# Where the background steps of a modulation stand, and which engine normalises v, in a two-layer retention and gMLP backbone

## The chip, the cores and the metric

The kernel runs on one core of one Trainium2 chip. The metric is the device time of one execution in microseconds, as the median of several runs. Engines are called PE (TensorE, the matmuls), DVE (VectorE), ACT (ScalarE), POOL (GpSimd) and SP (SyncE, which issues most DMA loads). Each engine works through its own instructions in order and waits on semaphores for the others.

## The reference

512 latent tokens and 256 context tokens of width 1024 go through two layers. Layer 0 is a retention mixer with four heads (query and key width 256, value width 512) in both directions, in which latents read context and latents. Layer 1 is a gMLP with spatial gating. Only the latents are put out, after a last RMS norm.

```python
shift, scale, gate = split(silu(c) @ ada_w[i] + ada_b[i], 3)       # per layer, 1024 each
hx = rmsnorm(x, norm_g[i]) * (1 + scale) + shift
# layer 0: q, k, v, z = hx @ w_in; retention in both directions; out = (rmsnorm(o) * silu(z)) @ w_out
# layer 1:
u, v, z = hx @ w_in                                              # 2048 each
v = v - mean(v); v = v * rsqrt(mean(v * v) + eps) * vnorm_g
mixed = einsum('gij,bnjgc->bnigc', w_s, v in chunks of 128) + b_s
out = (u * mixed * silu(z)) @ w_out
x = x + gate * out
```

## The kernel before

Everything is float32. A product is made as three matmuls of rounded halves (`mm3`): an operand is cast by ACT to its high half and DVE subtracts that from the original to get the low half (`split`, tiles `hl` for weights, `ya` and `og` for activations, `ph`/`pl` for scores). So every weight tile of 128x1024 costs one ACT cast and one DVE subtraction before PE can use it. The 2x2 block products of the projections are further made by a scheme with seven sub-products instead of eight (names B11, T1, T2, B21, T3, B22, T4 in `SINGLE`; a T is a difference of two raw weight tiles, a DVE subtraction `raw<-raw` ahead of its split). `Stream` (the object `Q`) loads the raw tiles and makes the splits two products ahead of PE.

The stages, with their rough times in the profile: start and layer 0's modulation (to 60 us); the projections of layer 0, nine unpaired groups ("quads") `n` of seven products each after a first one and a pair (to 350 us); attention over four heads, each followed by its part of the output projection (to 561 us); the v projection of layer 1 (to 640 us), which spills v to DRAM; then eight gating quads `i` with u and z, with an output product `out1` behind every second one (to 901 us).

*Order.* PE's instructions keep the order of the text. On DVE and ACT the framework's scheduler orders them by its own costs, except those made inside `aside(...)` (line 812): these are pinned behind the instruction that the text has ahead of them on their engine. SP issues loads in an order that the scheduler sets, each one waiting for its tile to be free; a waiting load holds those behind it.

*Background pieces.* Layer 1's modulation needs four vectors that come from 1024x1024 blocks of its matrix: the gate of layer 0 (piece 0), shift (1), scale (2) and the gate of layer 1 (3). `ada_piece` (line 745) makes one: nine loads' worth of steps in which tiles `bg` of 512 KB are loaded a step ahead, DVE multiplies the first by a column (`ada_a<-bg,cpad`, a TENSOR_SCALAR) and adds seven more (SCALAR_TENSOR_TENSOR). `background` (line 781) runs the pieces one after the other; each takes twelve steps: 1 loads only, 2 to 9 have one DVE instruction of 128x1024, 10 is empty, 11 and 12 turn the row into columns (`columns`: two small matmuls, an ACT copy `cole`, four transposes, a DVE copy), or for piece 3 load the bias (11) and add two 128x512 parts (12). One call of `step()` makes one step.

Steps are called in three places: in the loop over the projection quads (lines 925 to 939: product `i` of 7; five per quad until three pieces are done), in `attend` (line 947; `i` counts score pairs with the value product two behind, 0 to 7; three per head) and in `project_out` (line 1037; three per head).

*A head.* `score` makes the scores of a pair of blocks into one of two PSUM tiles `tm`, DVE scales them by the decay (`pf`), ACT casts (`ph`), DVE subtracts (`pl`). `pv` multiplies by v. At the end of a half of the tokens `finish` takes squares and their root on ACT (`junk`, `ss`), a DVE reciprocal and two `gt`; `flip` transposes `gt` on PE and splits it into `og`. At `i == 6` PE makes the value product of the fifth pair and then the transposes of the first half; at `i == 7` the value product of the sixth pair.

*Gating.* `bn_stats` and `bn_aggr` give mean and variance `mv` of v by token; `rv` is 1/sqrt(var + eps) (line 1220). `load_vt` (line 1286) loads a 256-column piece of v in two tiles `vt` of 128x2x256 and normalises it, four DVE instructions of 128x256; it is called at T2 of a gating quad for the next quad. After B22, sixteen matmuls mix v over tokens, and `gate_f` (line 1296) makes the gated product `ya`.

Of the kernel before, what the change touches and what calls it, by code (L numbers as in the profile page):

```python
# [9 lines left out]
AF = mybir.ActivationFunctionType  # L10
ALU = mybir.AluOpType
AX = mybir.AxisListType

P = 128
# [5 lines left out]
NT = SEQ // P  # L20
# [47 lines left out]
def hybrid_kernel(ctx, tc, xT_d, cT_d, cv_d, sv_d, rows_d, ada0_d, adag_d, w_d, rope_d, dec_d, ws_d, id_d, out_d):  # L68
    nc = tc.nc
    pe, act, dve, sp = (Queue(tc, e) for e in (nc.tensor, nc.scalar, nc.vector, nc.sync))  # L70
# [11 lines left out]
    def st(shape, tag, dt=F32, bufs=1, name=None):  # L82
        return sb.tile(shape, dt, tag=tag, name=name or tag, bufs=bufs)
# [37 lines left out]
    def pt(shape=(P, 512), tag="ps"):  # L121
        return ps.tile(list(shape), F32, tag=tag, name="pst", bufs=6 if tag == "ps" else 2)
# [21 lines left out]
    def load(dst, src):  # L144
        sp.dma_start(dst, src)
# [290 lines left out]
    g1 = sv[:, 72:80]  # L436
# [304 lines left out]
    def bg_raw(tags):  # L741
        spot[0] += 1
        return st([P, 1024], tags[spot[0] % len(tags)], name="bg")

    def ada_piece(i, tag, tags):
        a = st([P, D], tag, name="ada_a")
        rows = []
        for k in range(KT + 1):
            if k < KT:
                rows.append(bg_raw(tags))  # L750
                load(rows[k], adag_d[8 * i + k])
            if k == 0:
                yield None
                continue
            r, c = rows[k - 1], cpad[:, k - 1, 0:1]
            if k == 1:
                dve.tensor_scalar(a, r, c, None, ALU.mult)
            else:
                dve.scalar_tensor_tensor(a, r, c, a, ALU.mult, ALU.add)
            yield None  # L760
        yield a
# [19 lines left out]
    def background():  # L781
        for i in range(4):
            a = None
            for a in ada_piece(i, *(("g1", ("g2", "g3")) if i < 3 else ("oA22", ("w2", "w3")))):
                if a is None:
                    yield
            yield
            if i == 0:
                yield from columns(a, gate0)
                dve.tensor_tensor(gate0, gate0, gateb0, ALU.add)  # L790
            elif i == 1:
                yield from columns(a, sh1)
                dve.tensor_tensor(sh1, sh1, adab1[:, 0, :], ALU.add)
                dve.tensor_tensor(shs, sh1[:, 0:4], sh1[:, 4:8], ALU.add)
            elif i == 2:
                yield from columns(a, gs1)
                dve.tensor_tensor(gs1, gs1, adab1[:, 1, :], ALU.add)
                dve.scalar_tensor_tensor(gs1, gs1, 1.0, g1, ALU.add, ALU.mult)
            else:
                gb = st([P, D], "g1", name="gateb1")  # L800
                load(gb, rows_d[0:1, :].partition_broadcast(P))
                yield
                for j in range(2):
                    pr = pt(tag="tm")
                    mm(pr, ones, a[:, j * 512:j * 512 + 512], start=True, stop=True)
                    dve.tensor_tensor(gb[:, j * 512:j * 512 + 512], pr, gb[:, j * 512:j * 512 + 512], ALU.add)
                Q.gate = gb
            yield i
# [113 lines left out]
    pieces = []  # L922
    qk0 = load_qk(0)
    v0 = load_v(0)
    for n, q in enumerate(QUADS[3:]):
        pr = project(q)
        for i, name in enumerate(SINGLE):
            pr.run(name, Q.get())
            if i % 2:
                popped()  # L930
            if 2 not in pieces and i not in (2, 4):
                pieces.append(step())
            if n == 5 and i % 2 == 0:
                aside(dec0)
            if n >= 6:
                aside(qk0)
            if n == 8:
                aside(v0)
# [8 lines left out]
    def attend(h, qs, vs):  # L947
        q, k, kc = qk.pop(h)
        v, z = vv.pop(h)
        dt = dts[h]  # L950
        og = [st([P, 2, 4, HS], tag, F32R, name="og") for tag in ("oS3", "oS4")]
        steps = [(hf, j) for hf in range(2) for j in range(0, NK, 2)]
        ph, po, pend = {}, {}, []

        def key(j):
            return (k[j // 2], j % 2) if j < NT else (kc, j - NT)

        def score(hf, j):

            p = pt(tag="tm")  # L960
            for o in range(2):
                src, jj = key(j + 1 - o)
                for m in range(2):
                    l = (src[:, 0, m, jj * P:jj * P + P], src[:, 1, m, jj * P:jj * P + P])
                    mm3(p[:, o * HS:o * HS + HS], l, (q[hf][:, 0, m, :], q[hf][:, 1, m, :]), m == 0, m == 1)
            j1 = j + 1
            s0 = hf * HS - P * j1 + P * (NT - 1) if j < NT else XW + hf * HS - P * (j1 - NT) + P * (NC_T - 1)
            base = dt[:, s0:s0 + HS]
            both = bass.AP(base.tensor, base.offset, [base.ap[0], (P, 2), (1, HS)])
            two = lambda x: x.rearrange("p (o t) -> p o t", o=2)  # L970
            a = t2("pf")
            dve.scalar_tensor_tensor(two(a), two(p), 1.0 / 16.0, both, ALU.mult, ALU.mult)
            hl = t2("ph", dt=F32R), t2("pl", dt=F32R)
            split(hl, a)
            ph[hf, j] = hl

        def pv(hf, j):
            if j == 0:
                po[hf] = [pt(), pt()]
            h, l = ph.pop((hf, j))  # L980
            src = v[j // 2]
            for jj in range(2):
                for t in range(2):
                    o = (1 - jj) * HS + t * P
                    mm3(po[hf][t], (h[:, o:o + P], l[:, o:o + P]), (src[:, 0, jj, :], src[:, 1, jj, :]),
                        j + jj == 0, j + jj == NK - 1)
            if j == NK - 2:
                finish(hf)

        def finish(hf):  # L990
            ss = st([P, 2], "ss", bufs=2)
            for t in range(2):
                act.activation(t2("junk"), po[hf][t], AF.Square, accum_out=ss[:, t:t + 1])
            act.activation(ss, ss, AF.Sqrt, bias=eps, scale=1.0 / 512)
            dve.reciprocal(ss, ss)
            gts = []
            for t in range(2):
                g = t2("gt")
                dve.scalar_tensor_tensor(g, po[hf][t], ss[:, t:t + 1], z[:, 2 * hf + t, :], ALU.mult, ALU.mult)
                gts.append(g)  # L1000
            pend.append((hf, gts))

        def flip():
            hf, gts = pend.pop(0)
            for fp in range(2):
                pq = pt()
                for b in range(2):
                    for t in range(2):
                        o = b * HS + t * P
                        pe.transpose(pq[:, o:o + P], gts[t][:, (2 * fp + b) * P:(2 * fp + b) * P + P], ident)  # L1010
                src = pq.rearrange("p (b t) -> p b t", b=2)
                split((og[hf][:, 0, 2 * fp:2 * fp + 2, :], og[hf][:, 1, 2 * fp:2 * fp + 2, :]), src)

        LAG = 2
        wo = load_wo(h)
        for i in range(len(steps) + LAG):
            if i < len(steps):
                score(*steps[i])
            if i >= LAG:
                pv(*steps[i - LAG])  # L1020
            aside(qs)
            if i > 4:
                aside(vs)
            if i == len(steps):
                flip()
            if (h, i) == (0, 2):
                sp.pinned = True
                for c in range(4):
                    load(acc[:, 2 * c:2 * c + 2, :], xT_d[:, 2 * c:2 * c + 2, :])
                sp.pinned = False  # L1030
            if i < 5:
                aside(wo)
            if i in (3, 5, 6):
                step()
        return og, flip

# [180 lines left out]
    mv = st([P, NT, 2], "mv")  # L1217
    for t in range(NT):
        dve.bn_aggr(mv[:, t, :], bns[:, t, :, :])
    rv = st([P, NT], "rv")  # L1220
    act.activation(rv, mv[:, :, 1], AF.Sqrt, bias=eps, scale=1.0)
    dve.reciprocal(rv, rv)

    o1 = [st([P, D], f"s{t}", name="o1") for t in range(NT)]
    ya = st([P, 4, 2, SEQ], "hc", F32R, name="ya")
# [60 lines left out]
    def load_vt(i):  # L1286
        vts[i] = []
        for th in range(2):
            v = t2("vt", (P, 2, HS))
            load(v, vt_d[i][:, 2 * th:2 * th + 2, :])  # L1290
            for t in range(2):
                n = 2 * th + t
                dve.tensor_scalar(v[:, t, :], v[:, t, :], mv[:, n, 0:1], rv[:, n:n + 1], ALU.subtract, ALU.mult)
            vts[i].append(v)

    def gate_f(f, pm, mine):
# [144 lines left out]
```

## Time and profile before

| | |
|---|---|
| times of the runs | 908.04, 906.09, 906.26 us; median 906.26 |
| span of the profiled execution | 908.2 us |
| busy in it | PE 884.4 us (97%), DVE 720.0 (79%), ACT 445.8 (49%), POOL 51.4 (6%) |
| mean DMA rate | 168 GB/s over the span |
| commonest instruction groups | DVE split `hl<-raw,hl` 195 times, 1219 ns each; ACT cast `hl<-raw` 195 times, 1050 ns each |

The profile was taken of one execution; its span lies 0.2 us from the slowest of the three times and 1.9 from the median. Rows of a timeline read: start in us, duration in us, engine, line, operation, out<-in, shape, count, and in brackets how long the engine stood idle ahead of it and whose instruction ended that. All instructions show line 54, a helper; the tile names tell which is which. Consecutive instructions overlap a little, so from start to start is shorter than the duration (a 1.28 us instruction of 128x1024 takes 1.19 to the next start). PEclk is the granted clock of PE, 1.00 being full.

### The profile page before, as it was taken

The numbers are of one execution on the slowest core, as the hardware profiler recorded it, in microseconds if no ns is written. First come the engines' busy times: TensorE is split into PE (matmuls) and PEld (weight loads), VectorE is DVE, ScalarE is ACT, GpSimd is POOL, SyncE is SP. The second block draws the span as 40 slices with busy tenths as digits, with TensorE's granted clock in tenths as the row PEclk, the third lists the DMA queues.
The fourth block names the chain that finished last, engine by engine and source line by source line (L and its number), as shares of the span: only waits on it lengthen the run. The fifth ranks groups of instructions, "written<-read, shape, count | busy, mean of one in ns | idle before, by whom it ended". The sixth has DMA issues, their size and how long they took to land.

```text
span 908.2 us, 16915 instructions
## 1 busy us (share of the span) xinstructions
PE 884.4 (97%) x6872; PEld 839.3 (92%) x6872; DVE 720.0 (79%) x1024; ACT 445.8 (49%) x683; POOL 51.4 (6%) x88
## 2 busy tenths in 40 slices
PE   8999999999999999999999999999999999999986
PEld 7899999999999999998989898999999899899875
DVE  3689967698689876888677669999899478689975
ACT  5564634434445435626263558654445444353334
POOL 0001201101101011000000001111000000000000
PEclk9999999999999999999999999999999999999999
DMA  9933957467477458758253611636335035128002
GB/s 338 399 121 109 320 194 255 153 191 223 154 237 239 140 183 316 255 161 260 79 184 118 209 47 59 215 96 211 118 117 187 24 116 187 44 96 283 19 24 93
DMA packets 76782, 153.81 MB, mean 169 GB/s; under 512 B 7840, under 2 KB 34592, under 8 KB 76704
## 3 DMA queue, kind: packets, MB, share of 16 engines
q1 hardware_dynamic: 69840, 130.70, 44.2%
q0 software_dynamic: 6720, 22.03, 6.4%
q8 instruction: 54, 0.88, 0.4%
q14 instruction: 24, 0.20, 0.1%
q10 hardware_dynamic: 144, 0.01, 0.0%
HBM read 128.58 MB, written 24.12 MB: 168 GB/s over the span
## 4 chain that ended last, share of the span: by engine, by line
PE 67%; DVE 19%; DMA 5%; ACT 4%; issue 4%; SPq 1%; DVEq 0%; ACTq 0%
PE pst L54 67%; DVE hl L54 6%; DMA raw<-in_w_dram 3%; DVE raw L54 3%; DVE ya L54 2%; DVE o L54 2%; DVE snap L54 1%; SPq L54 1%; DMA vt<-vt 1%; DMA xq<-in_xT_dram 1%; ACT hl L54 1%; DVE f L54 1%; DVE pf L54 1%; ACT junk L54 1%; DVE oS L54 1%
## 5 line engine op out<-in xcount | busy, mean ns | idle before, releaser
L54 DVE TENSOR_TENSOR hl<-raw,hl 128x1024 fp32r<-128x1024 f32 x195 | 236.0, 1219 | 68.0 <-ACT hl L54 67.8
L54 ACT CAST hl<-raw 128x1024 fp32r<-128x1024 f32 x195 | 203.7, 1050 | 129.0 <-PE pst L54 71.2
L54 PE MATMUL pst<-oS,hl 128*128 128x256 f32 x1104 | 135.6, 282 | 4.6 <-DVE hl L54 3.9
L54 PE MATMUL pst<-hl,oS 128*128 128x256 f32 x1152 | 137.8, 281 | 2.0 <-DVE hl L54 1.8
L54 PEld LDWEIGHTS pst<-hl,oS 128*128 128x128 f32 x1152 | 135.8, 190 | 3.5 <-DVE hl L54 2.3
L54 PEld LDWEIGHTS pst<-oS,hl 128*128 128x128 f32 x1104 | 131.4, 190 | 6.9 <-ACT ya L54 3.7
L54 PE MATMUL pst<-oA,hl 128*128 128x256 f32 x936 | 117.5, 281 | 0.7 <-DVE snap L54 0.5
L54 PEld LDWEIGHTS pst<-oA,hl 128*128 128x128 f32 x936 | 112.2, 189 | 3.2 <-issue 1.3
L54 DVE TENSOR_TENSOR raw<-raw 128x1024 f32<-128x1024 f32 x92 | 111.4, 1218 | 1.2 <-DMA raw<-in_w_dram 0.5
L54 ACT COPY snap<-pst 128x512 f32<-128x512 f32 x92 | 53.9, 586 | 103.4 <-PE pst L54 102.9
L54 PE MATMUL pst<-hl,oA 128*128 128x256 f32 x816 | 98.6, 279 | 0.4 <-DVE snap L54 0.4
L54 PEld LDWEIGHTS pst<-hl,oA 128*128 128x128 f32 x816 | 96.3, 189 | 0.6 <-issue 0.6
L54 PE MATMUL pst<-og,hl 128*128 128x256 f32 x768 | 92.5, 281 | 0.0
L54 PEld LDWEIGHTS pst<-og,hl 128*128 128x128 f32 x768 | 90.4, 189 | 0.9 <-DVE acc L54 0.2
L54 PE MATMUL pst<-hl,ya 128*128 128x512 f32 x288 | 70.8, 399 | 2.7 <-DVE ya L54 2.7
L54 PEld LDWEIGHTS pst<-hl,ya 128*128 128x128 f32 x288 | 54.9, 192 | 15.2 <-DVE ya L54 3.1
L54 PE MATMUL pst<-v,ph 128*128 128x512 f32 x192 | 60.1, 395 | 0.0
L54 DVE TENSOR_TENSOR snap<-pst,snap 128x512 f32<-128x512 f32 x69 | 47.2, 684 | 3.9 <-PE pst L54 3.6
L54 ACT CAST ph<-pf 128x512 fp32r<-128x512 f32 x24 | 14.9, 621 | 67.1 <-DVE pf L54 66.7
L54 PE MATMUL pst<-hl,hc 128*128 128x256 f32 x384 | 47.4, 280 | 0.0
L54 PEld LDWEIGHTS pst<-hl,hc 128*128 128x128 f32 x384 | 46.0, 189 | 0.0
L54 PEld LDWEIGHTS pst<-v,ph 128*128 128x128 f32 x192 | 36.2, 188 | 7.3
(171 smaller groups left out, 970.3 us busy)
## 6 DMA issues: line engine op xcount, KB each, us to landing
raw<-in_w_dram SPq DMA_DIRECT2D x224, 256.0 KB, 4.4
bg<-in_adag_dram SPq DMA_DIRECT2D x32, 512.0 KB, 4.3
ada_w<-in_ada_dram SPq DMA_DIRECT2D x16, 512.0 KB, 8.7
raw<-in_w_dram SPq DMA_DIRECT2D x16, 512.0 KB, 4.3
bg<-in_dec_dram SPq DMA_DIRECT2D x12, 512.0 KB, 4.4
v<-snap POOLq DMA_DIRECT2D x16, 256.0 KB, 5.0
z<-snap POOLq DMA_DIRECT2D x16, 256.0 KB, 4.2
v<-v SPq DMA_DIRECT2D x8, 512.0 KB, 4.3
```

The source lines that it names most:

```text
L54: made = op(*args, **kw)
```

## The change

Five edits:

1. In `background`, the tiles `g1`, `g2`, `g3` serve pieces 0 and 1 only; piece 2 now uses `oA22`, `w2`, `w3`, as piece 3 does.
2. In the projection loop, steps are called at three products of a quad (0, 3, 5) instead of five (0, 1, 3, 5, 6), and until two pieces are done instead of three.
3. In `attend`, a step is called at every `i` from 2 to 7, six a head instead of three.
4. A new tile `nm` of 128x4 holds minus the mean times `rv`, by one DVE instruction.
5. `load_vt` normalises v by ACT (`Identity` with scale `rv` and bias `nm`) instead of DVE.

```diff
-            for a in ada_piece(i, *(("g1", ("g2", "g3")) if i < 3 else ("oA22", ("w2", "w3")))):
+            for a in ada_piece(i, *(("g1", ("g2", "g3")) if i < 2 else ("oA22", ("w2", "w3")))):
...
-            if 2 not in pieces and i not in (2, 4):
+            if 1 not in pieces and i in (0, 3, 5):
                 pieces.append(step())
...
-            if i in (3, 5, 6):
+            if i > 1:
                 step()
...
     dve.reciprocal(rv, rv)
+    nm = st([P, NT], "la", name="nm")
+    dve.scalar_tensor_tensor(nm, mv[:, :, 0], -1.0, rv, ALU.mult, ALU.mult)
...
-                dve.tensor_scalar(v[:, t, :], v[:, t, :], mv[:, n, 0:1], rv[:, n:n + 1], ALU.subtract, ALU.mult)
+                act.activation(v[:, t, :], v[:, t, :], AF.Identity, bias=nm[:, n:n + 1], scale=rv[:, n:n + 1])
```

In steps: before, pieces 0 to 2 end in the projection (at n = 7, i = 0), and piece 3 takes steps 1 to 3 in head 0, 4 to 6 in its output projection, 7 to 9 in head 1 and 10 to 12 behind it. After, piece 0 takes n = 0 to 3 and piece 1 n = 4 to 7; piece 2 takes steps 1 to 6 in head 0, 7 to 9 in its output projection and 10 to 12 in head 1; piece 3 takes 1 to 3 in head 1, 4 to 6 behind it and 7 to 12 in head 2.

## The prediction

> **What bounds the kernel now.** First the engine totals and PE's own waits, from the page and the list of waits.
>
> ```profile
> span 908.2 us, 16915 instructions
> PE 884.4 (97%) x6872; PEld 839.3 (92%) x6872; DVE 720.0 (79%) x1024; ACT 445.8 (49%) x683; POOL 51.4 (6%) x88
> ```
>
> ```profile
> PE pst L54 <- DVE hl L54: 5.7, 4, 2.0
> PE pst L54 <- DVE ya L54: 2.7, 1, 2.7
> PE pst L54 <- DVE pl L54: 1.7, 3, 0.7
> ```
>
> TensorE is the bound: 908.2 - 884.4 = 24 us idle in all, 10.1 of them in the three groups above, all released by DVE. Nothing in the change alters PE's work, only who prepares it, so only PE's waits can move: these and new ones. The prediction is a list of those waits. Second, the granted clock around the three longest waits (windows view: stretch, length, PE, PEld, DVE, ACT, POOL busy, PEclk, DMA share, GB/s), in stretches of 3.41 us.
>
> ```profile
> 221.44:224.85 3.41, 1.64 (x14) 1.44 (x14) 3.41 (x4) 1.60 (x3) 0.00 (x0) 1.00 0.74 258
> 224.85:228.26 3.41, 3.41 (x19) 3.41 (x18) 1.46 (x2) 0.00 (x0) 0.00 (x0) 0.50 0.83 190
> 658.34:661.75 3.41, 1.42 (x13) 1.25 (x12) 3.41 (x5) 3.41 (x6) 0.00 (x0) 1.00 0.00 0
> 661.75:665.16 3.41, 3.41 (x19) 3.41 (x18) 3.41 (x4) 0.83 (x1) 0.00 (x0) 0.50 0.23 61
> 747.08:750.49 3.41, 2.01 (x18) 1.83 (x17) 3.41 (x5) 3.41 (x6) 0.00 (x0) 1.00 0.00 0
> ...
> 880.21:883.62 3.41, 3.41 (x10) 2.63 (x9) 0.00 (x0) 0.00 (x0) 0.00 (x0) 0.50 0.00 0
> ```
>
> Where PE was idle for 3.41 - 1.64 = 1.77 us (224) or 1.99 (660), the next 3.41 us run at half clock and cost 0.5 x 3.41 = 1.7 us more; where it was idle 1.40 (749), PE has no such stretch after it. The third stretch, at 880.21, follows the ya wait of 2.7. The half-clock stretches begin at 224.85, 661.75 and 880.21, which lie 128 and 64 times 3.413 us apart: a free-running grid. So a wait of g us costs a stretch if more than some 1.6 us of it (my cut between 1.40 and 1.77) fall into one cell; for a random start that has the chance (g + 3.41 - 3.2)/3.41: 0.58 for 1.77, 0.65 for 1.99, 0.86 for 2.71, together 2.1 stretches an execution. The profiled one had three. The three times are 908.04, 906.09 and 906.26; the 1.8 us between the slowest and the median is about one stretch, so I read the median as an execution with two (an inference).
>
> The Trainium skill, page "TensorE: Matmul & The Clock Gate", in its rules for kernel authors, asks for no PE-idle gaps above about 3 us, one window of idle being what drops the clock. The trace disagrees: 1.77 us were enough. By that rule the sum below would have one stretch, behind the 4.35 us wait alone, and the kernel before none: 906.26 + 1.1 + 1.7 = 909.1, by chance the same time.
>
> **The change part by part.** *The projection: a step fewer on DVE ahead of a late split.* PE and DVE timelines around 224 us:
>
> ```profile
> 224.03 4.50 PE L54 MATMUL pst<-hl,oS 128*128 128x256 f32 x23 [1.77 <-DVE hl L54]
> ```
>
> ```profile
> 210.88 0.69 DVE L54 TENSOR_TENSOR snap<-pst,snap 128x512 f32<-128x512 f32 x1 [0.40 <-PE pst L54]
> ...
> 212.15 1.28 DVE L54 SCALAR_TENSOR_TENSOR ada_a<-bg,cpad,ada_a 128x1024 f32<-128x1024 f32 x1
> ...
> 218.02 1.27 DVE L54 SCALAR_TENSOR_TENSOR ada_a<-bg,cpad,ada_a 128x1024 f32<-128x1024 f32 x1
> ...
> 222.76 1.22 DVE L54 TENSOR_TENSOR hl<-raw,hl 128x1024 fp32r<-128x1024 f32 x1
> ```
>
> DVE last idles at 210.88 and is then back to back until the split that PE waits for. In between lie two ada_a instructions, 1.19 us each from start to start (212.15 to 213.35, 218.02 to 219.21). In the changed kernel's order neither is there: quad n=2 has no step at i=6, and the step at n=3, i=0 is the empty tenth one of a piece. The split ends 2.4 us earlier, the wait was 1.77: it goes, **-1.77**, and what is late next is PE itself, 0.6 us later. Everywhere else in the projection DVE has at most three steps a quad instead of five, and PE had no other wait there; I cost that at 0 because PE's queue of ready splits hides it. The DMA loads of the moved piece go along (eight, 512 KB each): on SP's queue they now come between the loads of attention, but behind the raw loads of the same head in the changed order, so 0; at worst one comes late by the 1.3 us of the DVE step that frees its tile.
>
> *Attention: the moved steps stand at the two head ends.* Head 0 before, on PE, DVE and ACT:
>
> ```profile
> 369.19 0.50 PE L54 MATMUL pst<-v,pl 128*128 128x512 f32 x1 [0.39 <-DVE pl L54]
> ```
>
> ```profile
> 359.67 0.68 DVE L54 SCALAR_TENSOR_TENSOR pf<-pst,dt 128x512 f32<-128x512 f32 x1
> ...
> 363.81 0.17 DVE L54 RECIPROCAL ss<-ss 128x2 f32<-128x2 f32 x1 [2.08 <-ACT ss L54]
> ...
> 367.08 0.69 DVE L54 SCALAR_TENSOR_TENSOR pf<-pst,dt 128x512 f32<-128x512 f32 x1
> 368.45 0.69 DVE L54 TENSOR_TENSOR pl<-pf,ph 128x512 fp32r<-128x512 f32 x1 [0.69 <-ACT ph L54]
> ...
> 369.66 0.75 DVE L54 TENSOR_SCALAR ada_a<-bg,cpad 128x1024 f32<-128x1024 f32 x1
> ```
>
> PE is through with the transposes at 368.80 and waits for pl of the last score pair. In the changed order a TENSOR_SCALAR of ada_a (0.66 from start to start) stands ahead of the pf at 359.67, and the whole chain behind it (ph, the squares, the square root, the gt) is serial, DVE waiting for ACT in it, so pf, ph and gt all come 0.66 later. Then an ada_a step (1.19) stands ahead of the pf at 367.08, which starts at 367.08 + 0.66 + 1.19 = 368.93. Last, both og splits (0.60 each from start to start) now stand between pf and pl, and ACT's two og casts ahead of ph: og at 369.53 and 370.13, pl at 370.73 instead of 368.45. PE starts 0.74 after pl, as before: 371.47. The wait is 2.7 instead of 0.39, **+2.3**. Head 2:
>
> ```profile
> 469.22 1.03 PE L54 MATMUL pst<-ident,gt 128*128 128x128 f32 x8
> 470.98 0.50 PE L54 MATMUL pst<-v,pl 128*128 128x512 f32 x1 [0.73 <-DVE pl L54]
> ```
>
> ```profile
> 468.14 0.68 DVE L54 SCALAR_TENSOR_TENSOR pf<-pst,dt 128x512 f32<-128x512 f32 x1
> 469.10 1.23 DVE L54 TENSOR_TENSOR hl_e<-raw,hl_e 128x1024 fp32r<-128x1024 f32 x1 [0.28 <-ACT hl_e L54]
> 470.24 0.69 DVE L54 TENSOR_TENSOR pl<-pf,ph 128x512 fp32r<-128x512 f32 x1
> ```
>
> The hl_e split leaves this place; an ada_a step comes ahead of pf (469.33) and the og splits ahead of pl. ACT casts og only when the transposes are out (469.22 + 0.5, and some 0.25 from PE to ACT, my estimate: 470.0), so og ends on DVE at 471.85 and pl starts there, 1.6 later than 470.24: wait 2.35, **+1.6**. The two earlier steps of that head lie in DVE idle time and hide. Head 1 gets only the 128x8 pieces of gs1 ahead of pl: 0 to 0.2. Bounds for the two heads: below, 0.7 each (the og splits alone, were pf on time); above, one more ada_a step, 1.2 each.
>
> *Gating: v by ACT.*
>
> ```profile
> L54 DVE TENSOR_SCALAR vt<-vt,mv,rv 128x256 f32<-128x256 f32 x32 | 11.6, 408 | 13.8 <-DMA vt<-vt 13.8
> L54 ACT ACTIVATE f<-f,sh,gs 128x256 f32<-128x256 f32 x16 | 8.3, 590 | 1.4 <-DVE f L54 1.4
> ```
>
> DVE loses 32 instructions, 11.6 us, and up to 13.8 us of waiting for the vt transfer; ACT gets 32 of the form of the second row (the same function, with bias and scale columns), which run at 0.50 us a piece back to back, 2.1 a quad. The one tiny instruction for nm is nearer to the 0.17 of the reciprocal than to 0.4: hidden. Now ACT waits for the transfer, and the hl cast queued behind it. Where that costs is the first quad:
>
> ```profile
> 637.47 1.37 DVE L54 TENSOR_SCALAR vt<-vt,mv,rv 128x256 f32<-128x256 f32 x4
> 638.77 2.35 DVE L54 TENSOR_TENSOR hl<-raw,hl 128x1024 fp32r<-128x1024 f32 x2
> ...
> 646.45 1.41 DVE L54 TENSOR_SCALAR vt<-vt,mv,rv 128x256 f32<-128x256 f32 x4 [2.73 <-DMA vt<-vt]
> 647.78 1.22 DVE L54 TENSOR_TENSOR hl<-raw,hl 128x1024 fp32r<-128x1024 f32 x1
> ```
>
> ```profile
> 640.92 0.86 SPq L54 DMA_DIRECT2D vt<-vt  x2
> ```
>
> ```profile
> 660.60 2.77 PE L54 MATMUL pst<-oS,hl 128*128 128x256 f32 x16 [1.99 <-DVE hl L54]
> ```
>
> The loads are issued at 640.92 behind a raw load that waits for the split of 638.77; that split comes 1.2 earlier, so issue at 639.7 and, with the 5.5 us they took (640.92 to 646.45), landing at 645.2. ACT: 2.1 for v, 1.05 for the cast: the split of 647.78 starts at 648.4, 0.6 late. Then the changed order puts one more split (1.14) and one ya (0.60) ahead of the T2 split that PE waits for: 2.35 late, wait 4.35, **+2.35**. Elsewhere DVE is freer. The waits of PE before:
>
> ```profile
> 749.44 2.98 PE L54 MATMUL pst<-oS,hl 128*128 128x256 f32 x24 [1.40 <-DVE hl L54]
> ...
> 762.85 3.00 PE L54 MATMUL pst<-oA,hl 128*128 128x256 f32 x24 [0.49 <-DVE snap L54]
> ```
>
> ```profile
> 735.96 0.74 DVE L54 TENSOR_SCALAR vt<-vt,mv,rv 128x256 f32<-128x256 f32 x2 [0.67 <-DMA vt<-vt]
> ...
> 748.08 1.22 DVE L54 TENSOR_TENSOR hl<-raw,hl 128x1024 fp32r<-128x1024 f32 x1
> ```
>
> At 749, DVE no longer stands at the transfer that landed at 735.96. ACT does: v until 736.96, the cast behind it until 738.0. In the changed order the split of that cast, a raw subtraction (1.14), the accumulation (0.60) and seven gating instructions up to 0.74 (about 3.3 together, by the same kind of rows) stand ahead of the T2 split, which so starts near 744.4 instead of 748.08 and is out before PE wants it at 749.44 - 1.40 = 748.04: -1.40. At 762, the accumulation that PE waits for no longer stands behind v: -0.49. The waits at 815 (0.55) and 878 (2.71, the row of ya above) are of the same kind; the first goes (-0.55), the second shrinks until the products of PE release the last gate, which I put at 1.0 (0 to 1.7). Together **-3.4**.
>
> **Sum**: -1.77 + 2.3 + 1.6 + 2.35 - 3.4 = +1.1 of waiting. Half-clock stretches, by the chance above: 0.85 (2.7), 0.75 (2.35), 1 (4.35) and 0.56 (1.7, the tail): 3.2 against 2.1, +1.8. On the profiled execution with its three, 908.2 + 1.1 = 909.3; on the median of the runs 906.26 + 1.1 + 1.8 = 909.1, which is the forecast.
>
> **The rivals.** *ACT held by vt in other quads too*: the loads come no earlier, and at 749 and 815 the casts wait as the first one does: 1.1 + 1.4 + 0.55 more, 912.1. For it: 13.8 us of DVE waits on these transfers exist. Against: ACT is busy 49% of the span, DVE 79%. *The wait at 224 stays*, being that of a transfer or a cast: +1.77 and 1.0 of stretches, 911.9; this is also the way in which the change would not do what it moves work for. Against: DVE was never idle from 211 on. *The grid misses the new waits*: same waits, two stretches as before, 907.4. *Not slower*: vt1 lands before ACT is through with the cast ahead of it (642.7). Then the split of 647.78 starts at 645.9, 1.9 early, the wait at 660 stays near 1.85 instead of 4.35, and 2.5 and 0.6 of stretch go: 906.0. It decides from a landing 2.5 us sooner than I assume; other vt loads took
>
> ```profile
> DMA to landing us min/median/max: 2.3/4.3/7.3
> ```
>
> so it can be. *Faster*: that, and the head ends at their lower bound (2.5 less) with a stretch fewer: about 902 to 904.
>
> **How the numbers follow.** Forecast 0.46; ACT held 0.12; 224 stays 0.08; grid misses 0.16; vt early 0.10; faster 0.08. A measurement of this kernel tells 0.2%, 1.8 us, from no change: below 904.4 or above 908.1. The forecast spreads by a stretch, so a little of it lies within: slower 0.60, same 0.27, faster 0.13. The range leaves out most of the faster case and the top of the held one: 904.3 to 911.9.
>
> **What would show it.** Right: no wait and full clock at 224; waits of over 2 us for pl at the ends of heads 0 and 2 and not of 1; the wait behind the first gating quad over 4 us; none at 749, 762 and 815. Wrong: a pl wait below 1 us, an ACT that never waits for vt, or PEclk 1.00 behind the new waits.

## The result, and the profile after

The changed kernel takes **909.99 us** (median of 20 runs, 904.48 to 912.53; one disturbed run of 2017.82 is left out of this range and of the ratio, and without it the median is 909.90), the kernel before 906.26 on the same chip (20 runs, 901.17 to 910.03). The ratio is **1.0032**, interval 1.0019 to 1.0045: slower by 1.7 to 4.1 us. (The ratio is not the quotient of the two medians, which differ by 3.7.) A second set on another chip (e8 below) gave 1.0042 (1.0024 to 1.0059). A run's time is 1.8 us above its span, so the profiled execution of before is its 910.03, the slowest of the 20, and that of after its 912.03: from profile to profile +2.0.

Engine totals of the changed kernel (the page), then the list of PE's waits (total us, times, longest):

```profile
span 910.2 us, 16910 instructions
...
PE 885.3 (97%) x6872; PEld 840.1 (92%) x6872; DVE 710.4 (78%) x993; ACT 461.6 (51%) x715; POOL 51.5 (6%) x88
```

```profile
PE pst L54 <- DVE pl L54: 4.3, 2, 2.2
PE pst L54 <- ACT hl L54: 4.2, 1, 4.2
PE pst L54 <- DVE ya L54: 2.7, 1, 2.7
...
PE pst L54 <- DVE hl L54: 1.1, 2, 0.7
```

DVE lost 9.6 us of work, ACT got 15.8, and PE's longest wait is now put down to ACT. The DVE splits `hl`, which held PE for 5.7 us before, hold it for 1.1. The same waits by place, in the timeline of PE:

```profile
296.73 1.53 PE L54 MATMUL pst<-oS,hl 128*128 128x256 f32 x11 [0.66 <-DVE hl L54]
...
366.13 0.79 PE L54 MATMUL pst<-v,pl 128*128 128x512 f32 x1 [2.16 <-DVE pl L54]
...
469.90 0.50 PE L54 MATMUL pst<-v,pl 128*128 128x512 f32 x1 [2.16 <-DVE pl L54]
...
664.70 2.69 PE L54 MATMUL pst<-oS,hl 128*128 128x256 f32 x11 [4.24 <-ACT hl L54]
...
867.03 2.24 PE L54 MATMUL pst<-oS,hl 128*128 128x256 f32 x17 [0.42 <-DVE hl L54]
...
881.63 2.93 PE L54 MATMUL pst<-hl,ya 128*128 128x512 f32 x6 [2.70 <-DVE ya L54]
```

No wait is left at 224, 749, 762 and 815, nor in head 1 (0.59 before). In order: -1.77 (224), +0.66, +1.77 (head 0), -0.59, +1.43 (head 2), -0.41 (587), +2.24 (first gating quad), -1.40, -0.49, -0.55, +0.42, and 0 at the tail: **+1.3** of waiting. The rest is the clock. PE's windows after, cut on the 3.41 us grid (stretch, length, PE, PEld, DVE, ACT, POOL busy, PEclk, DMA share, GB/s):

```profile
362.55:365.96 3.41, 1.42 (x11) 1.04 (x9) 3.35 (x5) 2.39 (x5) 0.00 (x0) 1.00 0.75 249
365.96:369.37 3.41, 3.24 (x8) 2.57 (x9) 2.51 (x4) 0.23 (x1) 0.00 (x0) 0.50 0.90 308
...
468.35:471.77 3.42, 1.87 (x8) 1.57 (x9) 2.70 (x5) 1.62 (x4) 0.00 (x0) 1.00 0.88 320
471.77:475.18 3.41, 3.41 (x16) 2.25 (x15) 1.13 (x3) 2.85 (x7) 0.00 (x0) 1.00 0.46 137
659.50:662.91 3.41, 0.96 (x9) 0.77 (x7) 3.41 (x5) 2.89 (x5) 0.00 (x0) 1.00 0.00 0
662.91:666.33 3.42, 1.63 (x7) 1.66 (x8) 3.42 (x4) 1.80 (x3) 0.00 (x0) 0.50 0.01 2
666.33:669.74 3.41, 3.41 (x17) 3.41 (x17) 1.63 (x2) 0.00 (x0) 0.00 (x0) 0.50 0.79 241
...
881.36:884.78 3.42, 3.15 (x7) 2.49 (x8) 0.81 (x2) 0.00 (x0) 0.00 (x0) 0.50 0.00 0
```

Head 0's wait falls with 1.99 us (3.41 - 1.42) into one cell, and the next cell runs at half clock. Head 2's wait is as long, but the grid cuts it into 0.61 and 1.55, and the clock stays. The wait of 4.24 costs two cells, though PE stands idle for half of the first. In PE's working time at half clock: 3.24 + 1.63 + 3.41 + 3.15 = 11.4 us, half of it lost, 5.7; before it was 3 x 1.7 = 5.1. So 1.3 + 0.6 = 1.9 of the 2.0 is accounted for; the other differences (the start, PE's pace, the time behind its last matmul) are below 0.6 us each and nearly cancel. Between the medians the clock's part is larger: the mean granted clock of a run is 0.992 in the median of the 19 runs of after and 0.995 to 0.996 in three sets of 23 to 32 runs of before (e8's set, on one chip: 0.9925 against 0.996), and 0.0035 x 908 = **3.2 us** of the 3.7. This is an estimate: the clocks are given to 0.001, which is 0.9 us, and the mean also counts half clock in which PE had no work, some 2 us in both profiles.

Where the waits of the two heads come from, on DVE (head 0, then head 2):

```profile
354.18 0.75 DVE L54 TENSOR_SCALAR ada_a<-bg,cpad 128x1024 f32<-128x1024 f32 x1
354.84 0.68 DVE L54 SCALAR_TENSOR_TENSOR pf<-pst,dt 128x512 f32<-128x512 f32 x1
...
362.25 1.28 DVE L54 SCALAR_TENSOR_TENSOR ada_a<-bg,cpad,ada_a 128x1024 f32<-128x1024 f32 x1
363.44 0.69 DVE L54 SCALAR_TENSOR_TENSOR pf<-pst,dt 128x512 f32<-128x512 f32 x1
364.19 1.29 DVE L54 TENSOR_TENSOR og<-pst,og 128x512 fp32r<-128x512 f32 x2
365.39 0.68 DVE L54 TENSOR_TENSOR pl<-pf,ph 128x512 fp32r<-128x512 f32 x1
...
467.96 1.29 DVE L54 TENSOR_TENSOR og<-pst,og 128x512 fp32r<-128x512 f32 x2 [0.60 <-ACT og L54]
469.16 0.68 DVE L54 TENSOR_TENSOR pl<-pf,ph 128x512 fp32r<-128x512 f32 x1
```

In head 0 an `ada_a` step stands ahead of each of the two `pf`, and in both heads both `og` splits stand ahead of `pl`; PE goes on 0.74 after `pl` in both, as forecast. And the first gating quad, on ACT, SP's queue and DVE:

```profile
639.48 2.08 ACT L54 ACTIVATE vt<-vt,nm,rv 128x256 f32<-128x256 f32 x4 [1.25 <-DVE nm L54]
641.93 1.05 ACT L54 CAST hl<-raw 128x1024 fp32r<-128x1024 f32 x1
...
647.09 2.08 ACT L54 ACTIVATE vt<-vt,nm,rv 128x256 f32<-128x256 f32 x4 [2.67 <-DMA vt<-vt]
649.07 1.04 ACT L54 CAST hl<-raw 128x1024 fp32r<-128x1024 f32 x1
```

```profile
641.90 0.86 SPq L54 DMA_DIRECT2D vt<-vt  x2
```

```profile
650.14 1.23 DVE L54 TENSOR_TENSOR hl<-raw,hl 128x1024 fp32r<-128x1024 f32 x1 [3.87 <-ACT hl L54]
```

ACT waits 2.67 us for a load, then spends 2.0 on v, and the cast queued behind both keeps DVE idle for 3.87.

### The profile page after: what moved, and what is told of

The parts are those of the page before. It is cut to its first block, busy times and chain, and to the rows that moved or that the text cites. A ratio compares the mean times of both kernels' runs of the same rounds, so it can differ in the third digit from the quotient of the medians.

```text
span 910.2 us, 16910 instructions
## 1 busy us (share of the span) xinstructions
PE 885.3 (97%) x6872; PEld 840.1 (92%) x6872; DVE 710.4 (78%) x993; ACT 461.6 (51%) x715; POOL 51.5 (6%) x88
## 4 chain that ended last, share of the span: by engine, by line
PE 81%; DVE 10%; ACT 3%; DMA 2%; issue 2%; SPq 1%; DVEq 0%; ACTq 0%
PE pst L54 81%; DVE hl L54 3%; DVE raw L54 2%; DVE o L54 2%; DVE ya L54 1%; DMA xq<-in_xT_dram 1%; ACT hl L54 1%; SPq L54 1%; DMA vt<-vt 1%; ACT f L54 1%; DMA raw<-in_w_dram 0%; ACT junk L54 0%; DVE snap L54 0%; DMA xs<-x 0%; DVE bns L54 0%
```

## The experiments

Each set of runs shares its runs of the kernel before, on one chip: e1 to e4 (before 907.17), e5 to e8 (907.55), e9 to e12 (906.25). Ratios are to that kernel, with a 95% interval.

### Each half of the change alone: e1 and e2

e1 is the kernel before with edits 4 and 5 only, e2 with edits 1 to 3 only. e1:

```diff
+    nm = st([P, NT], "la", name="nm")
+    dve.scalar_tensor_tensor(nm, mv[:, :, 0], -1.0, rv, ALU.mult, ALU.mult)
...
-                dve.tensor_scalar(v[:, t, :], v[:, t, :], mv[:, n, 0:1], rv[:, n:n + 1], ALU.subtract, ALU.mult)
+                act.activation(v[:, t, :], v[:, t, :], AF.Identity, bias=nm[:, n:n + 1], scale=rv[:, n:n + 1])
```

> The kernel before with v normalised by ACT alone (edits 4 and 5). Theory (the order on ACT at the first quad holds PE): waits of PE at 224 and the three small pl waits as before (1.77, 0.39, 0.59, 0.73); the wait behind the first gating quad 4.2 instead of 1.99, released by the cast behind v; those at 749, 762 and 815 gone. Sum of waits +0.2, a stretch of half clock more: 0 to +2.5 us against before. Rival (ACT has no room for 16 us of v, in any quad): waits for ACT in most quads, +4 us or more.

907.41 us, ratio 0.9992 (0.9978 to 1.0006): no difference. PE's timeline of e1:

```profile
223.94 4.37 PE L54 MATMUL pst<-hl,oS 128*128 128x256 f32 x23 [1.94 <-DVE hl L54]
...
661.68 4.60 PE L54 MATMUL pst<-oS,hl 128*128 128x256 f32 x24 [3.66 <-ACT hl L54]
```

The wait at 224 is still there, the one at 661 has grown from 1.99 without any step moved and is now released by ACT, and those at 749, 762 and 815 are gone: v on ACT gives back about as much as it takes.

> The steps moved alone (edits 1 to 3), v on DVE as before. Theory: no wait at 224, 2.2 at the ends of heads 0 and 2, none at that of head 1, gating as before (1.99, 1.40, 0.49, 0.55): waits +1.5, stretches +0.6 on the mean: +1 to +3.5 us. Rival (moving DMA loads and DVE work into attention costs nothing, all the loss is v's): -1.8 to -3 us, the wait at 224 and its stretch gone.

e2 has the other three edits of the change (pieces, three steps a quad, every `i` from 2 on in `attend`) and v on DVE. 908.29 us, 1.0014 (1.0001 to 1.0027). The wait at 224 is gone, heads 0 and 2 wait 2.16 each, as in the whole change, and the first gating quad waits 0.63 only, where 1.99 as before was expected. So the head waits belong to the steps and the quad's to ACT.

### The step at i = 4: e3

```diff
-            if i > 1:
+            if i in (2, 3, 5, 6, 7):
```

> The changed kernel with steps in attention at i = 2, 3, 5, 6, 7, without i = 4; piece 3 ends in the output projection of head 2. Theory (the step at i = 4, pinned behind the gt on DVE, stands ahead of the last pf and brings the og splits ahead of pl): waits for pl 0.4 to 0.8 at head 0 and about 1.2 at head 2 instead of 2.2 each, no half clock behind either: 2.4 less waiting, 3 to 5 us faster than the changed kernel, 0 to 2 faster than before. Rival (the moved work delays pl wherever it stands): waits for pl of 2 us or more, the time of the changed kernel.

The changed kernel without that step: 906.24 us, 0.9988 (0.9973 to 1.0002), against 1.0032 and 1.0042 for the whole change. DVE at the end of head 0, then of head 2:

```profile
361.88 0.69 DVE L54 SCALAR_TENSOR_TENSOR pf<-pst,dt 128x512 f32<-128x512 f32 x1
363.26 0.69 DVE L54 TENSOR_TENSOR pl<-pf,ph 128x512 fp32r<-128x512 f32 x1 [0.69 <-ACT ph L54]
...
465.23 0.69 DVE L54 TENSOR_TENSOR og<-pst,og 128x512 fp32r<-128x512 f32 x1 [1.79 <-ACT og L54]
465.83 0.68 DVE L54 TENSOR_TENSOR pl<-pf,ph 128x512 fp32r<-128x512 f32 x1
```

In head 0 `pf` is back to follow the split, `og` no longer comes ahead of `pl`, and the wait falls from 2.16 to 0.19. In head 2 an `og` split still stands ahead of `pl` and DVE is idle ahead of it for 1.79 us: the wait (1.56) is that for ACT's cast of `og`, which the order now puts first. The step's own time is hidden there: in both kernels the first `og` split starts 1.26 us behind the first transpose (467.96 and 466.70 in the changed one, 465.23 and 463.97 here), when ACT's cast is done. The 0.6 by which the wait is shorter is the second `og` split, which no longer stands ahead of `pl`. So at head 0 it is the step, and at head 2 the order of `og`, that holds PE.

### v normalised late: e4

```diff
+    def norm_vt(i):
+        for th in range(2):
+            v = vts[i][th]
             for t in range(2):
                 n = 2 * th + t
                 act.activation(v[:, t, :], v[:, t, :], AF.Identity, bias=nm[:, n:n + 1], scale=rv[:, n:n + 1])
...
+            if name == "T4" and i < UZ - 1:
+                act.pinned = True
+                norm_vt(i + 1)
+                act.pinned = False
```

`load_vt` now only loads; ACT's work stands at T4, four products later in the text and, in the first quad, two weight casts later on ACT.

> The changed kernel with the ACT instructions of v pinned two products later, behind the casts that the transfer held. Theory: the wait behind the first gating quad falls from 4.2 to below 1 us, no half clock there: 3.3 less waiting and 2.6 of clock, 4 to 6 us faster than the changed kernel. Rival (the split is late for DVE's own order, a split and a ya ahead of it): the wait stays at 2 to 3 us, 1 to 3 faster.

904.17 us, 0.9962 (0.9944 to 0.998), with both head waits of 2.16 still there. ACT and PE in the first gating quad:

```profile
653.41 1.08 ACT L54 ACTIVATE vt<-vt,nm,rv 128x256 f32<-128x256 f32 x2
```

```profile
659.47 5.60 PE L54 MATMUL pst<-oS,hl 128*128 128x256 f32 x48
```

The cast that queued behind v is through at 647.82 now, v comes 5.6 us later and finds its data there, and PE runs through the place without a wait. The wait of 4.24 was one of order on ACT's queue, not of ACT's speed.

### The wait at 224: e5 and e9

Both are the kernel before with two steps left out, to be made later. e5 left out the two that the prediction named, e9 the two that are in fact there:

```diff
-            if 2 not in pieces and i not in (2, 4):
+            if 2 not in pieces and i not in (2, 4) and (n, i) not in ((2, 6), (3, 0)):
```

> The kernel before with two background steps skipped in the projection (n = 2, i = 6 and n = 3, i = 0), nothing else; pieces end two steps later. Theory (the wait at 224 is DVE's backlog of two ada_a steps): that wait and its half clock are gone, the rest as before: 1.8 to 3.5 us faster than before. Rival (the split waits for its raw transfer or for the cast): the wait stays, no change.

e5: 907.43 us, 1.0002 (0.9984 to 1.002), the wait still 1.94; the expectation was missed. Its DVE timeline holds both `ada_a` instructions in their old places, at 212.27 and 218.14. So the theory wasn't tested; the steps had been named wrongly. e9's line:

```diff
+            if 2 not in pieces and i not in (2, 4) and (n, i) not in ((3, 5), (3, 6)):
```

> The kernel before with the two background steps skipped that really stand ahead of the wait at 224 (n = 3, i = 5 and 6; in the run before this one the two skipped steps lay a quad earlier). Theory (DVE's backlog): the wait of 1.8 to 1.9 at 224 gone or below 0.7, the rest as before, 1 to 3 us faster. Rival (the split waits for a cast that PE or a transfer releases): the wait stays at 1.5 or more.

e9: 904.10 us, 0.9968 (0.995 to 0.9987). DVE and PE in the same place:

```profile
215.08 2.36 DVE L54 TENSOR_TENSOR hl<-raw,hl 128x1024 fp32r<-128x1024 f32 x2 [0.53 <-ACT hl L54]
```

```profile
224.20 2.88 PE L54 MATMUL pst<-hl,oA 128*128 128x256 f32 x24
```

With two instructions fewer DVE even has to wait for ACT, and PE passes 224 without a wait and at full clock. So it was DVE's backlog that made the wait.

### Idle filled, to price the clock: e6 and e10

PE gets products of `ones` whose result nobody reads, ahead of the three new waits (16, 16 and 34 calls in e6; 8, 8 and 12 in e10), so that the waits stay in the order and PE isn't idle:

```diff
+    def idle(n):
+        d = pt()
+        for _ in range(n):
+            mm(d[:, :P], ones, ones, start=True, stop=True, skip_group_check=True)
...
+                if h in (0, 2):
+                    idle(8)
...
+            if (i, name) == (1, "T2"):
+                idle(12)
```

> The changed kernel with matmuls of ones added on PE where it waits: 16 of 128x128 ahead of the last value product of heads 0 and 2, 34 ahead of T2 of the second gating quad; their result is not used. Theory (half clock follows idle of more than half a 3.41 us cell): the ends of the waits stay where they are, as DVE and ACT set them, but PEclk is 1.00 behind all three; 3 to 5 us faster than the changed kernel on the mean, for nothing but PE being kept busy. Rival (the waits cost only themselves, the clock drops for another reason): same time as the changed kernel, half clock as before.

> As the run with matmuls of ones, but with 8 at the heads and 12 at the quad (each takes two passes of 0.11 us, so 1.8, 1.8 and 2.6 us). Theory: the filled waits end where DVE and ACT end them, less than 1.6 us of idle is left in each, PEclk 1.00 behind all three: 2.5 to 4.5 us faster than the changed kernel. Rival: half clock behind some of them all the same, or the ends of the waits later: no gain.

e6: 916.24 us, 1.0099 (1.008 to 1.0118): too much filling. PE and DVE at head 0:

```profile
364.43 3.74 PE L54 MATMUL pst<-ones 128*128 128x128 f32 x32
367.93 0.48 PE L54 MATMUL pst<-v,pl 128*128 128x512 f32 x1
```

```profile
366.02 0.68 DVE L54 TENSOR_TENSOR pl<-pf,ph 128x512 fp32r<-128x512 f32 x1
```

A call is two matmuls of 0.11 us, so 16 calls last 3.5 us and end well after `pl`; all 66 calls are some 15 us of work, put into waits of 8.6 in all. The clock behind all three places is 1.00, but the time, 5 to 6 us above the changed kernel's where 3 to 5 below it was expected, tells nothing of the clock. e10: 905.46 us, 0.9989 (0.9972 to 1.0006), against 1.0032 and 1.0042 for the same order without the filling: some 3 to 5 us less, although PE gets its operands no sooner (at head 0 the transposes end at 364.38, and 2.16 us lie between them and the next value product, as in the changed kernel). PE at head 0 and the window around it:

```profile
366.54 0.50 PE L54 MATMUL pst<-v,pl 128*128 128x512 f32 x1 [0.37 <-DVE pl L54]
```

```profile
365.56:368.98 3.42, 3.05 (x17) 2.43 (x16) 3.32 (x5) 1.11 (x4) 0.00 (x0) 1.00 0.82 277
```

The mean clock of its runs is 0.998, against 0.992 of the changed kernel: 0.006 x 908 = 5.4 us. The clock behind the waits costs about as much as the whole change does.

### The changed kernel again: e8

No edit.

> The changed kernel itself, beside the others on one chip. Theory: 0.2 to 0.45% slower than before; the same three waits within 0.6 us, since the order of the instructions sets them, the landing of vt moving the third one; half clock behind some of them only, as the cells fall.

911.21 us, 1.0042 (1.0024 to 1.0059). The profiled execution of this one is its third fastest of 12 (908.51, span 906.7). Its PE timeline, and the cell in which the wait of head 0 ends:

```profile
366.60 0.51 PE L54 MATMUL pst<-v,pl 128*128 128x512 f32 x1 [2.16 <-DVE pl L54]
...
662.90 1.41 PE L54 MATMUL pst<-oS,hl 128*128 128x256 f32 x5 [2.78 <-ACT hl L54]
```

```profile
365.69:369.10 3.41, 2.50 (x11) 2.06 (x12) 3.33 (x6) 1.09 (x3) 0.00 (x0) 1.00 0.89 324
```

The wait of head 0 has the same 2.16 us, but the grid divides it into 1.24 and 0.92, and no half clock follows. That is chance of the grid. The quad's wait varies too: 2.78 here, 4.24 in the first profile. Counted from the start of one product of PE (641.20 here, 641.94 there), the loads are issued 0.7 us earlier here (640.47 and 641.90) and land 0.4 sooner (4.8 and 5.2 us after the issue), and PE comes to the wait 0.4 later (after 18.9 and 18.5 us): together the 1.5. What makes these three vary is not shown.

### Both repairs, and what each is worth: e7, e11 and e12

e7 is the changed kernel with the edits of e3 and e4. e11 is e7 with v back on DVE at T2 (the last edit of the diff undone, `nm` and `norm_vt` out). e12 is e7 with 5 calls of `idle` ahead of head 2's wait and 7 ahead of the last `ya`:

```diff
+                if h == 2:
+                    idle(pt(), 5)
...
+                if (p, hf, t, k) == (3, 0, 0, 3):
+                    pr[1] = pt()
+                    idle(pr[1], 7)
```

> The changed kernel without the step at i = 4 in attention and with v's ACT instructions two products later. Theory: both effects add: waits for pl of 0.4 and 1.2 to 1.6 us, none above 1 us in gating, half clock at most in the tail: 8 to 10 us faster than the changed kernel, 6 to 7 faster than before. Rival (one cover hides the other, the time comes back later): 5 us or less faster than the changed kernel.

> The steps of the faster version (no step at i = 4) with v on DVE as before. It tells what v on ACT with the later place is worth. Theory (v on ACT is a gain once no cast stands behind the transfer): 3 to 5 us slower than the version with both, waits in gating of 0.6 to 2.0, 0.6, 0.3 to 1.4, 0.2 to 0.5 again; about 2 us faster than before. Rival (v's engine does not matter, the steps are all): within 1 us of the version with both.

> The version with both, and matmuls of ones into the waits that are left: 5 ahead of the last value product of head 2, 7 in the tail's wait for ya. Theory: idle below 1.6 us in both, so no half clock: 0 to 2 us faster than the version with both, 7 to 9 faster than before, and a narrower spread of times. Rival (the version with both hardly meets half clock any more): the same time.

e7: **900.31 us, 0.9919** (0.99 to 0.9937). PE has two waits above 1 us behind the start, apart from one of 1.16 at the norm ahead of layer 1 that every kernel here has:

```profile
467.47 0.50 PE L54 MATMUL pst<-v,pl 128*128 128x512 f32 x1 [1.56 <-DVE pl L54]
...
869.72 2.57 PE L54 MATMUL pst<-hl,ya 128*128 128x512 f32 x10 [1.88 <-DVE ya L54]
```

Neither is followed by half clock in this profile. e11: 906.91 us, 1.0004 (0.9987 to 1.0022). So with the steps as in e7, v on ACT at its late place is worth 0.85% or 7.7 us, more than the 3 to 5 expected, and the steps of e7 alone are not the 2 us faster than before that were expected. PE's waits in e11, and DVE's for the loads of v, show where the time is:

```profile
PE pst L54 <- DVE hl L54: 5.8, 6, 2.5
PE pst L54 <- DVE ya L54: 3.0, 1, 3.0
```

```profile
DVE vt L54 <- DMA vt<-vt: 15.9, 10, 3.6
```

In the gating quads PE waits 6.0 us in e11 (seven waits from 0.20 to 2.50) and nowhere over 0.2 in e7, and for the last `ya` 1.2 more. At its place in the change v on ACT cost some 0.2 to 0.3% (1.0032 and 1.0042 against e2's 1.0014), but these intervals overlap, and e1 shows no cost. e12: 899.04 us, 0.9916 (0.9898 to 0.9934), within the interval of e7, where a small gain was expected. The median of the mean clocks is 0.9965 in e7 and 0.998 in e12, so filling had 1.4 us at most to win, less than the intervals (1.7 us to each side) can tell. e7 is the better version, 0.8% faster than the kernel before and 1.1 to 1.2% faster than the changed one.

## Why the prediction was right

The forecast was 909.1 against 909.99, slower, by the mechanism that it named: new waits of PE at the head ends and behind the first gating quad, against others that go, and the half clock behind them. That it came within 1 us is in part luck, since several terms were off by 0.4 to 1.4 us in both directions. Point by point:

- **224 goes (-1.77)**: right, and e9 shows the cause. The steps were named wrongly: the two `ada_a` instructions are made at n = 3, i = 5 and 6, not at n = 2, i = 6 and n = 3, i = 0; after the change the first of these places holds the small instructions of `columns` and the second has no step. The backlog had been read from the timeline, so the sum stood; only e5 was led astray by the wrong names.
- **Head 0 (+2.3)**: 2.16 instead of 2.7, +1.77. The `og` splits and the `ada_a` step ahead of the last `pf` are there. The 0.66 of the TENSOR_SCALAR is there as well, but it delays nothing: the `pf` behind it starts 9.13 us ahead of the end of PE's transposes in both kernels (354.84 to 363.97, 359.67 to 368.80). Counted from that end, DVE is 0.46 us earlier than before from the first `pf` of the head on (342.04 and 347.33), and ACT's cast ahead (351.95 and 357.44), which had waited 0.34 for its raw load before, is 0.66 earlier. Why the head begins earlier on DVE is not shown.
- **Head 2 (+1.6)**: 2.16 instead of 2.35, +1.43, by the order of `og` as forecast; ACT's cast starts 0.64 us behind the first transpose (466.70 to 467.34), where some 0.75 had been estimated. **Head 1 (0 to +0.2)**: -0.59, since a step left the place ahead of its `pf`; not seen.
- **First gating quad (wait 4.35)**: 4.24, and the terms hold. The forecast put its times on the axis of before, but PE came to this place 1.85 us later (660.46 instead of 658.61). Counted from PE, the loads were issued 0.9 us earlier than before (641.90 and 640.92) where 1.2 was forecast, and took 5.2 us instead of 5.5, two small errors that cancel; the split behind the cast (650.14 and 647.78) starts 0.5 late where 0.6 was forecast, and one more split and a `ya` stand ahead of the split that PE waits for (663.34 and 659.24), the 1.74 of the forecast. That the wait is longer on ACT than on DVE, and why, is shown by e1, e2 and e4. Its size is not steady: 2.78, 2.98, 3.66 and 4.24 in the profiles with v on ACT at T2 (e8, e3, e1 and after).
- **749, 762 and 815 (-2.4)**: right. **The tail (-1.0)**: wrong, 2.70 as before. Two small waits (0.66, 0.42) were not forecast.
- **Sum of waits, +1.1**: +1.3 in the profile, and nearly nothing in e8, whose quad waits 1.46 less.
- **Half clock, +1.8**: the step that was mis-sized. The mean clocks say 3.2 us. The mechanism was right (grid, 3.41 us, 1.7 us a stretch, chance by length) and e10 shows it, but the cut was put at 1.6 us of idle in a cell. The end of PE's work shows the phase of the grid in every trace: the clock drops on a boundary (in after at 908.67, 159.0 cells of 3.413 us behind the stretch at 365.95; the nine profiles with half clock ahead of the end all give whole numbers). So the 14 profiles can be sorted by idle per cell, for cells that ran at full clock themselves:

| idle in one cell | where | next cell |
|---|---|---|
| 1.55, 1.60, 1.65, 1.69, 1.75, 1.75 | after head 2, e8, e11 (two), e5, e6 | 1.00 |
| 1.77 | before at 224 | 0.50 |
| 1.81 | e9 | 1.00 |
| 1.88 to 3.15, nineteen | | 0.50 |

The cut is near 1.78, just over half a cell, and not sharp: 1.77 us dropped the clock and 1.81 did not. Behind a cell at half clock less idle was enough for another: 1.79 us (after, in the cell from 662.91) and 0.74 (e3, from 657.45) were followed by half clock again, 0.55 (e8, from 877.68) and less were not; two cells are too few for a rule. With the cut of 1.78 the chance of a wait g up to 3.4 us is (g + 3.41 - 2 x 1.78)/3.41: 0.54 for 1.99 and 0.75 for 2.71, and for 1.77 between 0 and 0.47, so 1.3 to 1.8 stretches before; 2 x 0.59, 0.75 and 1.2 (the wait of 4.24, which can fill two cells) make 3.1 after. That is 1.4 to 1.8 stretches more, by this estimate 2.3 to 3.1 us, nearer to the 3.2 than the forecast's 1.8. The 1.77 at 224, which the forecast counted with 0.58, sat on the edge, and the new waits lie above it.

The windows that carry the cut, of e11: a wait of 2.50 that ends at 682.03 leaves PE idle for 1.69 of the first cell and 0.81 of the second, and the clock stays.

```profile
677.80:681.22 3.42, 1.73 (x16) 1.53 (x14) 3.42 (x6) 2.27 (x4) 0.00 (x0) 1.00 0.00 0
681.22:684.63 3.41, 2.60 (x23) 2.63 (x24) 3.41 (x4) 2.79 (x4) 0.00 (x0) 1.00 0.02 5
```

The Trainium skill, page "TensorE: Matmul & The Clock Gate", section "Why this matters for your kernels", puts the limit at PE-idle gaps of about 3 us, one window of idle. The runs disagree: 1.77 and 1.88 us in one cell were enough, and waits about as long as the limit, 2.99 (e9) and 3.05 us (e11), were not when they lay across a boundary. By that rule only the gap of 4.24 would have cost in after.

Of the rivals, *ACT held in other quads* and *224 stays* are refuted by the waits that are gone; *the grid misses* is e8's profile at the two heads, one execution among others; *vt early* is the quad's spread, which is real (2.78 to 4.24) and not enough.

What stays open: why DVE stands earlier in head 0, what makes the quad's wait vary, and how much idle keeps the clock at half once it is there.

## What to carry to other kernels

Work moved to an engine with room is hidden or not by what is queued behind it: the same ACT instructions gained nothing where a cast waited behind them and their load (e1; on top of the steps some 2 us slower, within overlapping intervals), and 7.7 us where they came later. The gaps of PE are to be priced twice, by their length and by the clock, for which not the length but the part in one 3.41 us cell counts: in this kernel gaps under some 1.7 us cost nothing more, while a gap of 2.16 was followed by a stretch that costs 1.7 more in four of eight cases. And before a step is blamed, its place in the code is to be checked by its instruction, not counted out.

## What the runs showed of the hardware

- The clock's grid runs free of the program: the same wait of 2.16 us was followed by half clock in head 0 of three profiles (after, e2, e4) and not in a fourth (e8). It is a part of the spread of a kernel's runs (901 to 910 us before): in the three other sets of before the runs of higher mean clock are the shorter ones (correlation -0.57, -0.64 and -0.80). e7 and e12, with few waits over 1.7, spread over 2.1 us only, but in six runs each.
- PE's pace at full clock is not quite the same in each execution: the same 24 matmuls of 128x256 took 2.72 us from start to start in after (641.94 to 644.66) and 2.83 in e8 (641.20 to 644.03). No run shows why.
- The same pair of loads of 256 KB landed 4.2 (e1), 4.8 (e8) and 5.2 us (after) after the issue.
- ACT's instruction with a scale and a bias column took 592 ns for 128x256 against DVE's 408, and the kernels with v on ACT at its late place (e4, e7) are the faster ones all the same.
